# Strassen's seven block products in place of eight in a two-layer decoder's second input projection

## The chip, the core and the metric

The kernel runs on one core of one Trainium2 chip, as one program. The metric is the device time of one execution in microseconds (us). The kernel before was timed in three runs.

## What is computed

The reference is a two-layer decoder trunk on 512 tokens of width 1024, in float32. Each layer normalizes its input, mixes it (layer 0 by attention, layer 1 by a gated linear recurrence), adds the normalized result, and adds a gated embedding. The change lies where layer 0 ends and layer 1 begins:

```
gate = sigmoid(h @ ple_w_gate[0]);  h = h + (p[0] @ ple_w_proj[0]) * gate      # end of layer 0
u = rms_norm(h, norm_pre[1])                                                   # layer 1
q, fl, inp, g = split(u @ rec_w_in)          # four projections, each 512 x 1024 @ 1024 x 1024
... recurrence over chunks with q, fl, inp -> o ...
y = (rms(o) * out_gain * silu(g)) @ rec_w_out
```

`inp` (called i or `it` in the kernel) and `g` are wanted with tokens on the partitions; q and fl with channels on the partitions.

## The kernel before

All activations live in SBUF as eight tiles of 128 channels by 512 tokens. A float32 product is made of three matmuls: each operand is split into a rounded part (hi, type fp32r) and the rest (lo), and `three` (lines 138 to 142) adds hi·hi, lo·hi and hi·lo in one PSUM bank. A weight comes as a 512 KB chunk of 128 x 1024: `fetch` (L112) loads it by DMA from the SP queue into `w_raw`, a pool of three buffers; `load_w` (L117) splits it: ACT writes `w_hi` (the cast, L273), then DVE subtracts to get `w_lo` (L274). `w_hi` and `w_lo` have two buffers each, so a chunk can be split when the matmuls on the chunk two before it are done.

The end of layer 0 is `layer_tail` (L339). Its gate projection makes eight output tiles: `lin_c` (L175) makes the first four together, `lin_a` (L152) the others one after the other, 24 matmuls each, each with one chunk of `wgA`. Behind each output tile o comes `gated` (L387): ACT's sigmoid (`sgm`), DVE's product and sum into `h[o]`, and then `nxt(o)` (L401): the next layer's input is scaled by its norm's gain and split into `xg` (the tiles `b2h`, `b2l`; ACT L281, DVE L282), and ACT squares `h[o]` and DVE adds it to `ss_acc` (L222 to L230) for the norm.

Layer 1 begins with the projections i and g (lines 731 to 744). `lin_b_tok` (L188) makes a quarter of one: 512 tokens by 512 columns, four banks of 128 tokens, over eight channel tiles, with `xg` as the stationary operand and the weight as the moving one (128 x 512): 96 matmuls and four chunks of `wB1`. There are four such calls: two for i, two for g. The norm's factor per token is applied when the banks are emptied (`evac_tok`, L731). It comes from `Stat.rstd` (L248: four tiny matmuls, L236; DVE; then GpSimd's power, L252, on the engine called POOL) and is spread over the partitions for the channel-major copy `u` of the input by `spread` (L255: four matmuls, L259). `u` is made by `scaled_norm` (L285) on DVE and ACT under the products, and serves q and fl later.

Every engine runs its own instructions strictly in the order of its queue. Most of that order is chosen by a scheduler when the program is built. Under `tc.manual_schedule(engines={PE})` the order of PE's queue is that of the source. In the kernel before, the projections i and g stand outside of such a block; in the changed kernel they stand inside.

## Time and profile before

| what | value |
|---|---|
| median of three runs | 673.51 us (672.4 to 673.66) |
| the profiled execution's own time | 672.09 us |
| its span, first to last instruction | 670.3 us |
| busy share of the span: PE / DVE / ACT / POOL | 98% / 65% / 50% / 6% |
| granted TensorE clock, mean | 1.000 |
| chain that ended last: PE / DVE | 92% / 5% |
| projections i and g, first matmul of the first to last of the last | 352.89 to 441.68 us |

A busy share is a mean over stages with different limits. PE's matmuls are pipelined: one is shown as some 0.39 us long, but the next one begins before it ends, so that a stream is to be read by the distance between starts.

### The profile page before, as it was taken

To read this page: it belongs to the slowest core of one execution; us is meant where nothing else is said; L and a number is where in the kernel's file an instruction comes from. 1 tells how busy PE (TensorE), PEld (TensorE's weight loads), DVE (VectorE), ACT (ScalarE), POOL (GpSimd) and SP (SyncE) were. 2 spreads that over 40 slices of the span, in tenths; PEclk is the share of its full clock that TensorE was granted. 3 is DMA by queue.
4 is the path that set the end of the run, shared out by engine and by line. 5 is a ranking of instruction groups with operands and counts; after the bars stand their busy time and mean duration, and the time that the engine had idled before them with its cause. 6 is when DMAs were issued, how large, how long until landed. Compare 5 with 4: busy or idle time off the path is not lost.

```text
span 670.3 us, 8922 instructions
## 1 busy us (share of the span) xinstructions
PE 657.3 (98%) x3226; PEld 548.4 (82%) x3226; DVE 434.6 (65%) x893; ACT 336.9 (50%) x656; POOL 39.6 (6%) x45
## 2 busy tenths in 40 slices
PE   8999999999999998999999999999999998999996
PEld 5888888888888877888888888888888887888886
DVE  7596223888888897337694372329888888233963
ACT  6457223766767685444563453344445455433431
POOL 1102200000000061001000110000010000001000
PEclk9999999999999999999999999999999999999999
DMA  7311326655555573221223223321122124122121
GB/s 283 130 64 65 128 95 189 165 151 133 153 139 139 150 230 100 95 95 37 92 92 125 84 79 109 135 68 64 63 70 89 63 93 135 56 96 95 58 107 59
DMA packets 26578, 73.22 MB, mean 109 GB/s; under 512 B 3808, under 2 KB 4192, under 8 KB 26528
## 3 DMA queue, kind: packets, MB, share of 16 engines
q1 hardware_dynamic: 26528, 72.59, 33.9%
q8 instruction: 27, 0.44, 0.3%
q14 instruction: 23, 0.19, 0.1%
HBM read 57.76 MB, written 2.10 MB: 89 GB/s over the span
## 4 chain that ended last, share of the span: by engine, by line
PE 92%; DVE 5%; ACT 1%; DMA 1%; issue 1%; POOL 0%; SPq 0%; ACTq 0%; DVEq 0%; POOLq 0%
PE psA L140 17%; PE psA L141 17%; PE psA L142 17%; PE psB L140 7%; PE psB L142 7%; PE psB L141 7%; PE psB L638 2%; PE psB L653 1%; PE psB L615 1%; PE psB L652 1%; PE psB L614 1%; PE psA L182 1%; PE psA L183 1%; PE psA L185 1%; PE psB L183 1%; PE psB L185 1%
## 5 line engine op out<-in xcount | busy, mean ns | idle before, releaser
L274 DVE TENSOR_TENSOR w_lo<-w_raw,w_hi 128x1024 fp32r<-128x1024 f32 x91 | 111.6, 1228 | 104.1 <-ACT w_hi L273 98.8
L140 PE MATMUL psA<-b1h,w_hi 128*128 128x512 f32 (+1 forms) x384 | 154.6, 403 | 0.0
L142 PE MATMUL psA<-b1l,w_hi 128*128 128x512 f32 (+1 forms) x384 | 148.5, 387 | 0.0
L141 PE MATMUL psA<-b1h,w_lo 128*128 128x512 f32 (+1 forms) x384 | 148.2, 386 | 0.2 <-DVE w_lo L274 0.2
L273 ACT CAST w_hi<-w_raw 128x1024 fp32r<-128x1024 f32 x92 | 96.2, 1047 | 62.4 <-PE psB L141 42.1
L142 PEld LDWEIGHTS psA<-b1l,w_hi 128*128 128x128 f32 x384 | 72.1, 188 | 15.1
L140 PEld LDWEIGHTS psA<-b1h,w_hi 128*128 128x128 f32 x384 | 72.3, 188 | 12.9 <-ACT sgm L389 0.7
L141 PEld LDWEIGHTS psA<-b1h,w_lo 128*128 128x128 f32 x384 | 72.5, 189 | 12.6 <-DVE w_lo L274 0.6
L140 PE MATMUL psB<-w_hi,b2h 128*128 128x512 f32 x144 | 56.3, 392 | 0.0
L142 PE MATMUL psB<-w_lo,b2h 128*128 128x512 f32 x144 | 56.1, 389 | 0.0
L141 PE MATMUL psB<-w_hi,b2l 128*128 128x512 f32 x144 | 56.1, 389 | 0.0
L621 ACT ACTIVATE pp<-pp,nm 128x128 f32<-128x128 f32 (+3 forms) x64 | 36.2, 565 | 23.0 <-DVE nm L619 22.2
L619 DVE CUSTOM_DVE_ANT_0 pp<-psB,cmask 128x128 f32<-128x128 f32 (+3 forms) x64 | 30.7, 480 | 14.5 <-PE psB L638 11.2
L230 DVE TENSOR_TENSOR ss_acc<-ss_acc,sq 128x512 f32<-128x512 f32 x26 | 17.9, 690 | 28.9 <-ACT sq L226 28.7
L140 PE MATMUL psA<-b2h,w_hi 128*128 128x512 f32 x80 | 31.8, 397 | 0.0
L142 PEld LDWEIGHTS psB<-w_lo,b2h 128*128 128x128 f32 x144 | 27.0, 188 | 5.7
L141 PEld LDWEIGHTS psB<-w_hi,b2l 128*128 128x128 f32 x144 | 27.1, 188 | 5.5
L140 PEld LDWEIGHTS psB<-w_hi,b2h 128*128 128x128 f32 x144 | 27.0, 188 | 5.5
L274 DVE TENSOR_TENSOR PTl<-psB,PTh 128x128 fp32r<-128x128 f32 (+3 forms) x64 | 30.8, 482 | 1.0 <-ACT PTh L273 0.8
L638 PE MATMUL psB<-ident,pp 128*128 128x128 f32 x160 | 28.4, 276 | 2.9 <-DVE pp L624 1.5
L142 PE MATMUL psA<-b2l,w_hi 128*128 128x512 f32 x80 | 31.2, 390 | 0.0
L141 PE MATMUL psA<-b2h,w_lo 128*128 128x512 f32 x80 | 31.2, 390 | 0.0
(228 smaller groups left out, 1217.5 us busy)
## 6 DMA issues: line engine op xcount, KB each, us to landing
w_raw<-in_wA_dram SPq DMA_DIRECT2D x40, 512.0 KB, 3.2
w_raw<-in_wB_dram SPq DMA_DIRECT2D x23, 512.0 KB, 3.3
w_raw<-in_wo_dram SPq DMA_DIRECT2D x16, 512.0 KB, 3.8
h<-in_xT_dram SPq DMA_DIRECT2D x16, 256.0 KB, 6.0
h<-kh SPq DMA_DIRECT2D x32, 128.0 KB, 2.3
w_raw<-in_wgC_dram SPq DMA_DIRECT2D x8, 512.0 KB, 3.2
w_raw<-in_wgA_dram SPq DMA_DIRECT2D x8, 512.0 KB, 3.3
h<-qh SPq DMA_DIRECT2D x16, 128.0 KB, 2.3
```

The source lines that it names most:

```text
L140: pe.matmul(out=out_ps, lhsT=sta[0], rhs=mov[0], start=start, stop=False)
L141: pe.matmul(out=out_ps, lhsT=sta[1], rhs=mov[0], start=False, stop=False)
L142: pe.matmul(out=out_ps, lhsT=sta[0], rhs=mov[1], start=False, stop=stop)
L182: pe.matmul(out=b, lhsT=hi[:, c], rhs=src[0][k], start=k == 0, stop=False)
L183: pe.matmul(out=b, lhsT=lo[:, c], rhs=src[0][k], start=False, stop=False)
L185: pe.matmul(out=b, lhsT=hi[:, c], rhs=src[1][k], start=False, stop=k == KT - 1)
L230: ve.tensor_tensor(out=self.acc, in0=self.acc, in1=sq, op=ALU.add)
L273: ins = ac.copy(dst_hi, src)
L274: eng.tensor_tensor(out=dst_lo, in0=src, in1=dst_hi.bitcast(F32), op=ALU.subtract)
L619: ve.tensor_tensor_reduce(out=pp[:, :W], in0=sc[:, :W], in1=cmask[:, S - W:S], op0=ALU.add, op1=ALU.min, scale=1.0, scalar=-NEG, accum_out=nm)
L621: ac.activation(out=pp[:, :W], in_=pp[:, :W], func=AF.Exp, bias=nm, scale=-1.0, accum_out=den)
L638: pe.transpose(out=tp[:, kt * P:(kt + 1) * P], in_=pp[:, kt * P:(kt + 1) * P], identity=ident)
```

## The change

1. i and g, each 512 x 1024 from 512 x 1024 times 1024 x 1024, are cut into 2 x 2 blocks (256 tokens, 512 channels, 512 columns) and made of seven block products in the scheme of Strassen in Winograd's form. Each `product` is 4 channel tiles x 2 halves of 128 tokens x 3 matmuls = 24 matmuls of 128 x 512; `token_major` calls it seven times, in the order p1, p6, p7, p5, p2, p4, p3, once for i and once for g.
2. The four sums of activation blocks (D, E, F, G) are made in `pair`, called by `nxt` behind output tiles 4 to 7 of the gate projection: two ACT multiplies (`un`), four DVE sums of 128 x 256 written into a `w_raw` buffer, and a split of the 128 x 1024 into `as0k` and `as1k`. For output tiles 0 to 3, `xg` is now made for 256 tokens alone.
3. Every product has two weight chunks of its own to split: 28 chunks in place of 16. Sums of weight blocks: b11 + b12 (`t1`, in `tsum0`) and b12 + b22 come from a load by SP with an accumulating DMA behind it from POOL (`summed`); two more sums per chunk pair are made by DVE (L809, L826).
4. The results are added up from PSUM into `it` and `sg` by DVE (L796, 14 additions of 128 x 512 per projection), and scaled in place by ACT.
5. `r1` and its spread are now made between p1 and p6 of i, in PE's written order.

The diff, without empty lines:

```diff
--- before.py
+++ after.py
@@ -336,8 +336,10 @@
             with first(o == KT - 1):
                 ac.activation(out=self.zg[o], in_=b, func=AF.Copy, scale=col(C_NPOST[self.layer] + o))
 
-    def layer_tail(layer, h, ah, zg, last=False):
+    def layer_tail(layer, h, ah, zg, pair=None):
+        last = pair is None
         st = ah.st = Stat()
         ah.zg, hm = zg, ah.mem
         for g in ah.begun:
@@ -399,8 +401,12 @@
             stn = Stat()
 
             def nxt(o):
-                split_scaled(xg[0][o], xg[1][o], h[o], col(C_NPRE[1] + o))
+                f = slice(0, S // 2 if o < 4 else S)
+                split_scaled(xg[0][o][:, f], xg[1][o][:, f], h[o][:, f], col(C_NPRE[1] + o))
                 stn.add(h[o])
+                if o >= 4:
+                    pair(h, o - 4)
 
         banks = lin_c(ws, hm)
         ws = [load_w(wgA[layer, o]) for o in range(2)]
@@ -706,13 +712,33 @@
         nc.sync.dma_start(h[k], xT[:, k, :])
     att.close()
     turn[1] = 4
-    xg, st = layer_tail(0, h, ah, slots("b3h", F32))
     l1 = ctx.enter_context(tc.tile_pool(name="l1", bufs=1))
+    sums = att.enter_context(tc.tile_pool(name="sums", bufs=1))
+    TH = S // 2
+    SM_D, SM_E, SM_F, SM_G = range(4)
+    a_sum = [[sums.tile([P, 4, TH], F32R, name=f"as{q}{k}") for k in range(4)] for q in range(2)]
+    def pair(h, k):
+        un = []
+        for b in (k, k + 4):
+            un.append(t2("un"))
+            ac.mul(un[-1], h[b], col(C_NPRE[1] + b))
+        a11, a21, a12, a22 = [x[:, i * TH:(i + 1) * TH] for x in un for i in range(2)]
+        raw = wp.tile([P, D], F32, name="w_raw", tag="w_raw")
+        sm = raw.rearrange("p (j t) -> p j t", t=TH)
+        ve.tensor_tensor(out=sm[:, SM_D, :], in0=a21, in1=a22, op=ALU.subtract)
+        ve.tensor_tensor(out=sm[:, SM_E, :], in0=sm[:, SM_D, :], in1=a11, op=ALU.subtract)
+        ve.tensor_tensor(out=sm[:, SM_F, :], in0=a11, in1=a21, op=ALU.subtract)
+        ve.tensor_tensor(out=sm[:, SM_G, :], in0=a12, in1=sm[:, SM_E, :], op=ALU.add)
+        split(a_sum[0][k], a_sum[1][k], sm)
+    xg, st = layer_tail(0, h, ah, slots("b3h", F32), pair)
 
 
     lmin = const.tile([P, 1], F32, name="lmin")
@@ -728,20 +754,105 @@
     it = slots("b3h", F32)
     sg = slots("b3l", F32)
     u = pair_big("b1")
-    def evac_tok(q, banks):
-        for t in range(NT):
-            ac.activation(out=(it, sg)[q // 2][2 * t + q % 2], in_=banks[t], func=(AF.Copy, AF.Silu)[q // 2], scale=r1[:, t:t + 1])
-    banks = lin_b_tok(wB1[0:4], xg, 0)
-    r1 = st.rstd()
+    def operand(kind, k):
+        if isinstance(kind, int):
+            return [a_sum[q][k][:, kind, :] for q in range(2)]
+        row, c = kind
+        return [xg[q][k + 4 * c][:, row * TH:(row + 1) * TH] for q in range(2)]
+    def product(kind, ws):
+        banks = [psB(), psB()]
+        for k in range(4):
+            w, f = ws[k // 2], slice(k % 2 * S, (k % 2 + 1) * S)
+            hi, lo = operand(kind, k)
+            for t in range(2):
+                c = slice(t * P, (t + 1) * P)
+                three(banks[t], (hi[:, c], lo[:, c]), (w[0][:, f], w[1][:, f]), k == 0, k == 3)
+        return banks
+    def block(m, i, j, c):
+        return wB1[8 * m + 4 * j + 2 * i + c]
+    def summed(dst, *aps):
+        nc.sync.dma_start(dst, aps[0])
+        for ap in aps[1:]:
+            gp.dma_start(dst, ap, accum_op=ALU.add)
+        return dst
+    tsum = [[(l1, sums)[q].tile([P, D], F32, name=f"tsum{q}{c}", tag=f"tsum{q}{c}") for c in range(2)] for q in range(2)]
+    CH = range(2)
+    def token_major(m, dst, between=None):
+        def C(i, j, t):
+            return dst[2 * (2 * i + t) + j]
+        def plus(i, j, bank, src, op=ALU.add):
+            for t in CH:
+                ve.tensor_tensor(out=C(i, j, t), in0=bank[t], in1=C(*src, t), op=op)
+        def end(i, j):
+            for t in CH:
+                q = 2 * i + t
+                ac.activation(out=C(i, j, t), in_=C(i, j, t), func=AF.Silu if m else AF.Copy, scale=r1[:, q:q + 1])
+        w = [load_w(block(m, 0, 0, c)) for c in CH]
+        t1 = [summed(tsum[0][c], block(m, 0, 0, c), block(m, 0, 1, c)) for c in CH]
+        p1 = product((0, 0), w)
+        w = []
+        for c in CH:
+            b22 = fetch(block(m, 1, 1, c))
+            ve.tensor_tensor(out=tsum[1][c], in0=t1[c], in1=b22, op=ALU.add)
+            w.append(load_w(None, raw=tsum[1][c]))
+        if between:
+            between()
+        for t in CH:
+            ac.copy(C(0, 0, t), p1[t])
+        p6 = product(SM_E, w)
+        w = [load_w(None, raw=summed(wp.tile([P, D], F32, name="w_raw", tag="w_raw"), block(m, 0, 1, c), block(m, 1, 1, c))) for c in CH]
+        plus(0, 1, p6, (0, 0))
+        p7 = product(SM_F, w)
+        w = [load_w(None, raw=t1[c]) for c in CH]
+        plus(1, 0, p7, (0, 1))
+        p5 = product(SM_D, w)
+        w = []
+        for c in CH:
+            b21 = fetch(block(m, 1, 0, c))
+            w.append(load_w(None, raw=b21))
+            ve.tensor_tensor(out=tsum[1][c], in0=tsum[1][c], in1=b21, op=ALU.add)
+        plus(1, 1, p5, (1, 0), ALU.subtract)
+        end(1, 1)
+        plus(0, 1, p5, (0, 1), ALU.subtract)
+        p2 = product((0, 1), w)
+        w = [load_w(None, raw=tsum[1][c]) for c in CH]
+        plus(0, 0, p2, (0, 0))
+        end(0, 0)
+        p4 = product((1, 1), w)
+        w = [load_w(block(m, 1, 1, c)) for c in CH]
+        plus(1, 0, p4, (1, 0))
+        end(1, 0)
+        p3 = product(SM_G, w)
+        plus(0, 1, p3, (0, 1))
+        end(0, 1)
+    r1 = None
     rb = []
-    banks1 = lin_b_tok(wB1[4:8], xg, 1, between=lambda: rb.append(spread(r1)))
-    evac_tok(0, banks)
-    for k in range(KT):
-        scaled_norm(u, k, h[k], C_NPRE[1], rb[0])
-    evac_tok(1, banks1)
-    for q in range(2, 4):
-        evac_tok(q, lin_b_tok(wB1[4 * q:4 * q + 4], xg, q))
+    def rstd1():
+        nonlocal r1
+        r1 = st.rstd()
+        rb.append(spread(r1))
+    with tc.manual_schedule(engines={PE}):
+        token_major(0, it, rstd1)
+        for k in range(KT):
+            scaled_norm(u, k, h[k], C_NPRE[1], rb[0])
+        token_major(1, sg)
+    att.close()
 
     y = pair_big("b2")
 
@@ -749,7 +860,7 @@
         pass
 
 
-    w_f0 = load_w(wA1[8], [l1.tile([P, D], F32R, name=f"w_f0{q}") for q in range(2)])
+    w_f0 = load_w(wA1[8], [l1.tile([P, D], F32R, name=f"w_f0{q}", tag=f"tsum0{q}") for q in range(2)])
 
     def general(rp):
 
@@ -1055,7 +1166,7 @@
     with tc.If(ok > 0) as cmp:
         with tc.tile_pool(name="rec", bufs=2) as rp:
             ah = bounded(rp)
-        layer_tail(1, h, ah, it, last=True)
+        layer_tail(1, h, ah, it)
     with cmp.Else():
         with tc.tile_pool(name="rec", bufs=2) as rp:
             general(rp)
@@ -1068,7 +1179,7 @@
         for o in EARLY:
             for _ in ah.early(o):
                 pass
-        layer_tail(1, h, ah, it, last=True)
+        layer_tail(1, h, ah, it)
 
 
 _INS = ["xT", "pT", "vec", "wfl", "wA0", "wB0", "wA1", "wB1", "wo", "wgC", "wgA", "wpl"]
```

How the order of the queues changes at the places that the prediction speaks of. In the names, b2h6 is the hi part of `xg` tile 6, `sgm` the sigmoid, h7 the tile of `h`, as02 and as12 the hi and lo part of the four sums of pair 2.

DVE, in the gate projection of layer 0, from the split of its third chunk to the split of the fourth and last. Before:

```order
L274 TENSOR_TENSOR w_lo_3568<-w_raw_3565,w_hi_3567 128x1024
L391 TENSOR_TENSOR h3_2997<-h3_2997,sgm_3531 128x512
L390 TENSOR_TENSOR sgm_3571<-sgm_3571,b3l4_3369 128x512
L391 TENSOR_TENSOR h4_2998<-h4_2998,sgm_3571 128x512
L282 SCALAR_TENSOR_TENSOR b2l3_3388<-h3_2997,vecs_73,b2h3_3380 128x512
L230 TENSOR_TENSOR ss_acc_3393<-ss_acc_3393,sq_3537 128x512
L274 TENSOR_TENSOR w_lo_3608<-w_raw_3605,w_hi_3607 128x1024
```

DVE, the last ten instructions of the same piece in the changed kernel:

```order
L230 TENSOR_TENSOR ss_acc_3407<-ss_acc_3407,sq_3591 128x512
L731 TENSOR_TENSOR w_raw_3598<-un_3594,un_3596 128x256
L392 TENSOR_TENSOR sgm_3636<-sgm_3636,b3l5_3385 128x512
L732 TENSOR_TENSOR w_raw_3598<-w_raw_3598,un_3594 128x256
L393 TENSOR_TENSOR h5_2999<-h5_2999,sgm_3636 128x512
L734 TENSOR_TENSOR w_raw_3598<-un_3596,w_raw_3598 128x256
L733 TENSOR_TENSOR w_raw_3649<-un_3645 128x256
L282 SCALAR_TENSOR_TENSOR b2l5_3404<-h5_2999,vecs_73,b2h5_3396 128x512
L274 TENSOR_TENSOR as10_3021<-w_raw_3598,as00_3017 128x1024
L274 TENSOR_TENSOR w_lo_3633<-w_raw_3630,w_hi_3632 128x1024
```

Five instructions stood between the two splits; now there are fifteen, among them the four sums and the split of pair 0, the first sum of pair 1 and the output tile 5 (h5).

ACT, from the sigmoid of the last output tile of the gate projection to the first weight casts of the projections behind it (`w_hi_3781` is the second chunk of `wB1` before; `w_hi_3808` and `w_hi_3814` are the two chunks of p1 now). Before:

```order
L389 ACTIVATE sgm_3679<-psA_3654 128x512
L273 CAST w_hi_3781<-w_raw_3779 128x1024
L281 ACTIVATE b2h7_3384<-h7_3001,vecs_73 128x512
L226 ACTIVATE sq_3685<-h7_3001 128x512
L273 CAST w_hi_3811<-w_raw_3809 128x1024
```

ACT in the changed kernel:

```order
L391 ACTIVATE sgm_3726<-psA_3701 128x512
L727 ACTIVATE un_3735<-h3_2997,vecs_73 128x512
L281 ACTIVATE b2h7_3398<-h7_3001,vecs_73 128x512
L273 CAST as02_3019<-w_raw_3694 128x1024
L226 ACTIVATE sq_3732<-h7_3001 128x512
L727 ACTIVATE un_3737<-h7_3001,vecs_73 128x512
L273 CAST as03_3020<-w_raw_3739 128x1024
L273 CAST w_hi_3808<-w_raw_3806 128x1024
L273 CAST w_hi_3814<-w_raw_3812 128x1024
```

Before, the first chunk's cast stood ahead of that sigmoid and the second right behind it; now both stand behind everything that the last output tile and the pairs 2 and 3 ask of ACT, and DVE's queue has the same order (the `w_lo` of p1 behind `as13`).

PE, from the last matmuls of p1 of i to the first of p6 (`ss_acc` and `rs` belong to `r1` and its spread):

```order
L142 MATMUL psB_3823<-w_lo_3815,b2h3_3394 128x512
L236 MATMUL psB_3862<-ones1_101,ss_acc_3407 128x1 x4
L259 MATMUL psB_3871<-ident_90,rs_3869 128x128 x4
L140 MATMUL psB_3880<-w_hi_3851,as00_3017 128x512
L141 MATMUL psB_3880<-w_hi_3851,as10_3021 128x512
```

The two groups of four now stand next to each other; before, 24 matmuls of a projection stood between them.

## Rows read from the trace of the kernel before

**Rows 1.** The page, part 1: busy us (share of the span) xinstructions.

```profile
PE 657.3 (98%) x3226; PEld 548.4 (82%) x3226; DVE 434.6 (65%) x893; ACT 336.9 (50%) x656; POOL 39.6 (6%) x45
```

**Rows 2.** Timeline of PE, gate projection and first matmuls of i: start, us, instruction.

```profile
344.73 0.39 PE L140 MATMUL psA<-b1h,w_hi 128*128 128x512 f32 x1
...
347.68 0.39 PE L141 MATMUL psA<-b1h,w_lo 128*128 128x512 f32 x1
...
352.66 0.39 PE L142 MATMUL psA<-b1l,w_hi 128*128 128x512 f32 x1
352.89 0.39 PE L140 MATMUL psA<-w_hi,b2h 128*128 128x512 f32 x1
...
353.34 0.39 PE L142 MATMUL psA<-w_lo,b2h 128*128 128x512 f32 x1
```

**Rows 3.** Two stretches: us; busy PE, PEld, DVE, ACT, POOL (instructions); clock, DMA, GB/s.

```profile
331.00:353.00 22.00, 22.00 (x98) 18.24 (x98) 21.50 (x33) 15.30 (x24) 0.00 (x0) 1.00 0.21 72
354.00:441.00 87.00, 87.00 (x393) 72.23 (x392) 32.56 (x41) 32.48 (x42) 3.82 (x6) 1.00 0.29 101
```

**Rows 4.** Timeline of DVE in the gate projection.

```profile
340.29 1.22 DVE L274 TENSOR_TENSOR w_lo<-w_raw,w_hi 128x1024 fp32r<-128x1024 f32 x1
341.43 0.68 DVE L391 TENSOR_TENSOR h<-h,sgm 128x512 f32<-128x512 f32 x1
342.03 0.68 DVE L390 TENSOR_TENSOR sgm<-sgm,b3l 128x512 f32<-128x512 f32 x1
...
343.36 0.75 DVE L282 SCALAR_TENSOR_TENSOR b2l<-h,vecs,b2h 128x512 fp32r<-128x512 f32 x1
344.02 0.69 DVE L230 TENSOR_TENSOR ss_acc<-ss_acc,sq 128x512 f32<-128x512 f32 x1
344.62 1.22 DVE L274 TENSOR_TENSOR w_lo<-w_raw,w_hi 128x1024 fp32r<-128x1024 f32 x1
```

**Rows 5.** Timeline of DVE: half-width instructions at the kernel's start and end.

```profile
32.13 0.88 DVE L282 SCALAR_TENSOR_TENSOR b3h<-psA,rs,b3h 128x256 fp32r<-128x256 f32 x2 [1.42 <-ACT b3h L281]
...
665.71 0.43 DVE L390 TENSOR_TENSOR sgm<-sgm,b3l 128x256 f32<-128x256 f32 x1 [1.99 <-ACT sgm L389]
```

**Rows 6.** Timeline of ACT, the gate projection's end.

```profile
353.09 0.60 ACT L389 ACTIVATE sgm<-psA 128x512 f32<-128x512 f32 x1 [0.62 <-PE psA L142]
353.58 1.04 ACT L273 CAST w_hi<-w_raw 128x1024 fp32r<-128x1024 f32 x1
355.18 0.73 ACT L281 ACTIVATE b2h<-h,vecs 128x512 fp32r<-128x512 f32 x1 [0.55 <-DVE h L391]
355.81 0.61 ACT L226 ACTIVATE sq<-h 128x512 f32<-128x512 f32 x1
```

**Rows 7.** PE's first matmuls (L92): ns min/median/max, first and last start; then the last.

```profile
L92 PE MATMUL psB<-idle x9: 379/634/634, 1.3 to 4.5; 128*128 128x512 bf16 x9
...
L92 PE MATMUL psB<-idle x2: 379/386/393, 4.2 to 4.5; 128*128 128x512 bf16 x2
```

**Rows 8.** Timelines of DVE and POOL: the norm factor of layer 1.

```profile
375.73 0.16 DVE L239 TENSOR_SCALAR ms<-psB 128x4 f32<-128x4 f32 x1 [4.14 <-PE psB L236]
...
375.97 1.93 POOL L252 TENSOR_TENSOR rs<-ms,mhalf 128x4 f32<-128x4 f32 x1 [71.13 <-DVE ms L239]
```

**Rows 9.** Chain of waits: the two groups of small matmuls (start, us).

```profile
374.91 0.79 PE psB L236 x8
...
381.30 0.89 PE psB L259 x8
```

**Rows 10.** Timelines of ACT and DVE: one chunk's split within the projections.

```profile
363.84 1.05 ACT L273 CAST w_hi<-w_raw 128x1024 fp32r<-128x1024 f32 x1 [4.34 <-PE psB L141]
...
364.92 1.22 DVE L274 TENSOR_TENSOR w_lo<-w_raw,w_hi 128x1024 fp32r<-128x1024 f32 x1 [4.17 <-ACT w_hi L273]
```

**Rows 11.** Weight loads into w_raw, 330 to 450 us: issue ns; us to landing.

```profile
L114 SPq DMA_DIRECT2D w_raw<-in_wB_dram x16: 327/328/338, 334.1 to 417.0; - x16
...
DMA to landing us min/median/max: 3.2/3.3/4.9
```

## The prediction

> **What bounds the kernel now.** I read the page first. PE is busy for 98% of the span [rows 1], and the chain that ended last is PE for 92% of it: fewer matmuls are worth their full time as long as PE is kept fed. Next, PE's timeline: 35 matmuls lie between the starts 344.73 and 352.66 [rows 2], so one matmul of 128 x 512 costs 0.2266 us, and the stream runs into i without a gap: last matmul of the gate projection at 352.66, first of i at 352.89. Then the stretches, which decide this case: under i and g DVE is busy for 32.56 of 87.00 us, but in the gate projection, where the change puts its sums, for 21.50 of 22.00 us [rows 3]. There DVE is as full as PE; only nobody waits for it yet. A mean share of 65% doesn't show that. All sums below are against this execution's own 672.09 us, which is 1.42 us under the median of the runs shown, 673.51.
>
> **What is saved.** i and g are 4 x 96 = 384 matmuls; the change makes them 14 x 24 = 336. 48 x 0.2266 = **10.9 us** less on PE, all of it on the path. The small matmuls of the norm (0.79 and 0.89 us [rows 9]) are the same in both.
>
> **The last tile of the gate projection: 4.5 us late.** Prices on DVE, from start to start [rows 4]: 1.14 us for a chunk's split (340.29 to 341.43), 0.60 for a sum of 128 x 512 (341.43 to 342.03), 0.66 for a scaled difference (343.36 to 344.02). At half width a scaled difference is 0.40 (two in 0.88, one being 0.48 long), and a sum, 0.43 long, is 0.35, since the next begins 0.08 before its end [rows 5]. Between the splits of the third and fourth gate chunk now stand six full sums (3.6), two full and one half scaled difference (1.7), five half sums (1.75) and the split of pair 0 (1.14): 8.2 us instead of 3.2. DVE also waits for ACT three times, each time for the product of what it has itself just made: for b2h4 some 0.9 us (0.73 long [rows 6], nothing between), for b2h5 and as00 about 0.25 each, since DVE has other work meanwhile. The fourth split so begins at 340.29 + 1.14 + 8.2 + 1.4 = 351.0 and ends 1.22 later, at 352.2. PE wanted it at 347.68 [rows 2]: 4.5 us. A smaller count for the hand-overs gives 3.1, twice the count 5.9.
>
> **The entry into i: 10.2 us more.** ACT's queue puts the two casts of p1 behind everything that tile 7 and the pairs 2 and 3 ask for, though p1 reads none of it. Followed by hand, with the sigmoid of tile 7 at 353.09 + 4.5 = 357.6 [rows 6]: sigmoid to 358.2; on DVE product, one half sum of pair 2 and the sum into h7, to 359.85; ACT then makes b2h7 (0.62 to the next start), as02 (0.95), the square (0.52) and un7 (0.69), to 362.65. DVE has by then split as12 (from 361.5) and added the square, and is free at 363.25. The sums D, E and G of pair 3 each need the one before: 3 x 0.43, to 364.55. ACT: as03 0.95, then the first cast of p1, to 366.55; DVE: as13 1.14 from 365.6, then the first `w_lo` 1.22, to 368.0. So p1's third matmul begins at 368.0 where it began at 353.34 [rows 2]: 14.7 us in all, 10.2 beyond the 4.5. PE has nothing else in its order. A floor that needs no hand-over: the new work of DVE, 16 half sums (5.6) and 4 splits (4.6) less 4 x 0.26 for the halved `xg` tiles, is 9.1 us in an engine that had 0.5 us to spare; its old work ended at 357.5 (the sum after the last scaled difference), so p1's first `w_lo`, last but one in the queue, can't be done before 357.5 + 9.1 - 1.1 = 365.5: 12 us.
>
> **Clock: 1.4 us.** PE stands still for some 9 us there. The granted clock is 1.00 in both stretches [rows 3] and PE never stood that long, so the price comes from the only cold start shown: the first nine matmuls begin 0.40 apart (1.3 to 4.5), at 634 ns, and the last two take 379 to 393 [rows 7]. Eight steps at 0.40 - 0.23: 1.4 us, between nothing (the clock holds) and 2.8 (it falls in the 4.5 us wait too).
>
> **The norm factor in the open: 2.2 us.** Between p1 and p6 PE makes the means, waits for DVE (0.16) and POOL's power (1.93 [rows 8]) with nothing in between, then spreads. Before, 24 matmuls of the stream stood there. On POOL the power stands behind the issue of an accumulating DMA; by my times that has half a microsecond to spare, so 0 to 1.5 more.
>
> **Weights within the products: 3.7 us.** A chunk now lasts 12 matmuls, 2.7 us, instead of 24. Its buffer's refill takes 2.3 us (363.84 to 366.14 [rows 10]) and `w_lo` is wanted two matmuls after `w_hi`, so it fits, with 0.8 to spare, where nothing stands ahead of it. I price 26 of the 28 chunks at nothing; the cover is that spare 0.8, and without it each costs up to one addition, 0.6. Two places in g don't fit. p6: its split waits behind DVE's sums, 0.8. p7: its b12 + b22 chunk finds its buffer free only in the middle of p1. From there to p7 are 36 matmuls, 8.2 us; in it go the load 3.3 [rows 11], POOL's issue about 1 (between SP's 0.33 [rows 11] and the power's 1.93), the accumulation L, the cast 1.05 and 0.9 for the split and hand-overs: L - 2.0 late. No row shows an accumulating DMA. From below it is a plain load, 3.3; from above three of them, 10, as it reads two places and writes one. I take 5, nearer the plain one, since the slowest plain load takes 4.9 [rows 11]: 2.9 us. In i the open norm factor gives the same chunk 3.9 us more: nothing, up to an L of 6. By the fit of the Trainium skill, page "DMA: Bandwidth & Descriptors", section "Anatomy of one DMA — SWDGE (gpsimd) path" (2.0 us and the bytes at 436 GB/s), 512 KB would land in 3.2 us, an estimate: the sum would be 1.8 less; no run here shows it yet.
>
> **Costed at nothing:** the first `tsum0` loads and accumulations, which can start when attention's buffers come free and are wanted 100 us later; 14 additions per projection from PSUM (0.60 each) on a DVE that was one third busy [rows 3]; the recurrence behind, which is as before.
>
> **Sum.** -10.9 + 4.5 + 10.2 + 1.4 + 2.2 + 3.7 = **+11.1**: 683.2 against 672.09, and 684.6 as a median.
>
> **Rivals.**
> 1. *Slow accumulation.* L is 10: p7 of g loses 5 more and p7 of i 3.9: 693.5. For: POOL must prepare these while DVE is nearly always busy. Against: it hits two products only. The Trainium skill, page "SBUF — State Buffer", section "Who interferes with whom", has GpSimd and DVE lock each other out of a shared port, which would delay a descriptor written by GpSimd; it excepts sums of two tensors, DVE's main work here, by inference only.
> 2. *Not slower: the gate projection absorbs the sums.* If half sums cost DVE next to nothing and ACT hands over at once, only four splits less the halved tiles remain, 3.5 us, and the entry costs 4 in place of 14.7, with no cold clock: -10.9 + 4 + 2.2 + 2 = -2.7, 670.8. It decides at an entry of about 5 us in all (10.9 less 2.2 and 3.7). Against it: 21.50 of 22.00 busy [rows 3], and p1's casts stand behind pair 3 whatever the durations.
> 3. *DVE binds in the products.* Per projection it has 14 splits, 4 weight sums and 14 additions: 16.0 + 4.6 + 8.4 = 29.0 us for 168 matmuls, 38.1 us; in i the eight tiles of u (0.66 + 0.60 each) make it 39.1. Then up to 0.6 more at each of 14 products, 8.4: 693.0. Against: in i the wait for the norm factor gives it room, and in g 9 us are free.
>
> **How the numbers follow.** Forecast 0.71, slow accumulation 0.13, DVE in the products 0.08, absorbed sums 0.08. Low end: entry 12.0, no cold clock, L at 3.3: -10.9 + 12 + 2.2 + 1.3 = +4.6, 678; a little under it, 677. High end: the first and third rival, 693.5 and 693.0: 694. Beyond lies their coming together, and below most of the second rival. Faster or slower means by over 0.2% (1.35 us), about what a measurement of this kernel can tell. The second rival holds faster 0.05 and same 0.03; the rest is slower, 0.92.
>
> **What would show it.** Right: the first matmul of p1 some 14 us after 352.9, with ACT's `w_hi` as its releaser, and behind it the `as` splits; a wait of about 4 us in the last gate tile; one of 2 us on `rs`; from the first matmul of i to the last of g some 86 us instead of 89; slower matmuls right after the long gap. Wrong: an entry under 5 us, or a clock of 1.00 with evenly spaced matmuls all through; waits of a microsecond at most products would be the third rival, two long ones on a weight cast behind a POOL transfer the first.

## The result and the profile after

The changed kernel takes 694.29 us (median of four runs, 692.15 to 695.04) against 673.59 for the kernel before (four runs, 672.40 to 673.97): a ratio of 1.0305, 95% interval 1.0277 to 1.0333, 20.7 us slower. The sign is the predicted one; the time is 9.7 us above the forecast and 0.3 us beyond the upper end of the range. The profiled execution took 692.15 us (span 690.4), 20.06 more than that of before.

The page of the changed kernel, parts 1 and 4, to be read beside [rows 1]:

```profile
PE 658.6 (95%) x3178; PEld 544.1 (79%) x3178; DVE 485.3 (70%) x961; ACT 358.5 (52%) x684; POOL 46.5 (7%) x53
...
PE 83%; DVE 9%; DMA 3%; ACT 3%; issue 2%; POOL 1%; SPq 0%; ACTq 0%; DVEq 0%; POOLq 0%
```

PE issues 48 instructions fewer, and yet its busy time has risen by 1.3 us: some matmuls last longer. PE's share of the chain fell from 92% to 83%, and what took its place are DVE, DMA and ACT, that is, waits. Where they lie shows in PE's timeline, against [rows 2] (start, us, instruction, idle time before it and what ended it):

```profile
347.34 0.39 PE L142 MATMUL psA<-b1l,w_hi 128*128 128x512 f32 x1
350.96 0.80 PE L140 MATMUL psA<-b1h,w_hi 128*128 128x512 f32 x1 [3.24 <-ACT w_hi L273]
...
352.41 0.79 PE L141 MATMUL psA<-b1h,w_lo 128*128 128x512 f32 x1 [0.65 <-DVE w_lo L274]
353.00 0.63 PE L142 MATMUL psA<-b1l,w_hi 128*128 128x512 f32 x1
353.43 0.63 PE L140 MATMUL psA<-b1h,w_hi 128*128 128x512 f32 x1
...
359.82 0.39 PE L142 MATMUL psA<-b1l,w_hi 128*128 128x512 f32 x1
...
369.45 0.79 PE L140 MATMUL psB<-w_hi,b2h 128*128 128x512 f32 x1 [9.25 <-ACT w_hi L273]
...
370.90 0.79 PE L142 MATMUL psB<-w_lo,b2h 128*128 128x512 f32 x1 [0.23 <-DVE w_lo L274]
...
377.63 0.95 PE L236 MATMUL psB<-ones,ss_acc 128*128 128x1 f32 x8
380.90 1.82 PE L259 MATMUL psB<-ident,rs 128*128 128x128 f32 x8 [2.32 <-POOL rs L252]
...
432.19 0.62 PE L140 MATMUL psB<-w_hi,as 128*128 128x512 f32 x1 [3.19 <-ACT w_hi L273]
...
433.45 0.79 PE L142 MATMUL psB<-w_lo,as 128*128 128x512 f32 x1 [0.21 <-DVE w_lo L274]
```

There are four places where PE stands: the last gate tile, the entry into i (9.25), the norm factor (2.32) and p7 of g (3.19). Behind each, the next matmuls start 0.43 apart instead of 0.2266 (353.00 to 353.43 above). The stretches, with the columns of [rows 3], show the same from the side of the clock:

```profile
348.00:358.00 10.00, 6.38 (x15) 4.68 (x16) 9.26 (x16) 7.95 (x12) 0.00 (x0) 0.66 0.00 0
358.00:370.00 12.00, 2.75 (x11) 2.00 (x10) 8.37 (x15) 6.60 (x9) 0.00 (x0) 0.76 0.27 87
370.00:375.00 5.00, 4.77 (x13) 3.27 (x12) 3.21 (x3) 0.43 (x2) 0.00 (x0) 0.56 0.81 255
382.00:385.00 3.00, 3.00 (x11) 2.48 (x10) 2.85 (x4) 1.21 (x2) 0.00 (x0) 0.56 1.07 208
385.00:400.00 15.00, 15.00 (x66) 12.10 (x65) 12.90 (x16) 6.82 (x8) 0.84 (x1) 1.00 0.54 162
432.00:436.00 4.00, 3.60 (x8) 2.37 (x9) 1.90 (x2) 1.18 (x2) 0.00 (x0) 0.57 0.51 154
```

The third column from the right is the mean granted clock: 0.56 to 0.66 behind the waits, a mean over the lower level (1.2 GHz) and the upper one (2.4 GHz), and 1.00 once PE has run on for a while. In the first of them DVE is busy for 9.26 of 10.00 us. PE waits there for ACT's cast of the last gate chunk (3.24 us) and for DVE's split of it (0.65), and that cast stands behind the cast of `as00`, which needs DVE's sums. The end of the gate projection's queues, timelines of ACT and of DVE, shows the order that the prediction followed by hand:

```profile
367.41 1.04 ACT L273 CAST as<-w_raw 128x1024 fp32r<-128x1024 f32 x1 [2.00 <-DVE w_raw L734]
368.36 1.99 ACT L273 CAST w_hi<-w_raw 128x1024 fp32r<-128x1024 f32 x2
```

```profile
368.49 1.23 DVE L274 TENSOR_TENSOR as<-w_raw,as 128x1024 fp32r<-128x1024 f32 x1 [1.11 <-ACT as L273]
369.63 2.35 DVE L274 TENSOR_TENSOR w_lo<-w_raw,w_hi 128x1024 fp32r<-128x1024 f32 x2
```

The last sum of pair 3 releases the cast of `as03`; behind it stand p1's two casts, and on DVE p1's splits behind `as13`. Put together from start to start, against the same matmuls of before (the stream of the gate projection is 0.12 us later in this execution; that is taken off):

| place | predicted us | measured us |
|---|---|---|
| 48 matmuls fewer | -10.9 | -10.9 |
| last gate tile, wait for `w_lo` (347.68 to 352.41) | +4.5 | +4.6 |
| slow matmuls behind it (to 360.05) | 0 | +2.4 |
| entry into i, to p1's third matmul (370.90) | +10.2 | +10.4 |
| slow matmuls in p1 (to 377.63) | +1.4 | +1.7 |
| norm factor in the open (to 382.37) | +2.2 | +3.1, of which 0.7 slow |
| slow matmuls in p6 of i | 0 | +1.1 |
| p6 of g | +0.8 | +0.9 |
| p7 of g, wait for the b12 + b22 chunk | +2.9 | +4.2 |
| slow matmuls in p7 of g | 0 | +1.2 |
| products on `as`, start to start 0.2333 | 0 | +1.1 |
| the rest of i and g, less 0.4 of small waits of before | 0 | +0.1 |
| sum | +11.1 | +19.9 |

From the first `w_f` matmul on (441.90 before, 461.97 after) nothing differs.

### The profile page after: what moved, and what is told of

Same layout as the page of the kernel before. It is cut to its first block, busy times and chain, and to the rows that moved or that the text cites. A ratio compares the mean times of both kernels' runs of the same rounds, so it can differ in the third digit from the quotient of the medians.

```text
span 690.4 us, 8993 instructions
## 1 busy us (share of the span) xinstructions
PE 658.6 (95%) x3178; PEld 544.1 (79%) x3178; DVE 485.3 (70%) x961; ACT 358.5 (52%) x684; POOL 46.5 (7%) x53
## 4 chain that ended last, share of the span: by engine, by line
PE 83%; DVE 9%; DMA 3%; ACT 3%; issue 2%; POOL 1%; SPq 0%; ACTq 0%; DVEq 0%; POOLq 0%
PE psA L141 15%; PE psA L140 15%; PE psA L142 15%; PE psB L140 6%; PE psB L142 6%; PE psB L141 6%; DMA w_raw<-in_wB_dram 2%; PE psB L644 2%; DVE w_lo L274 1%; PE psB L659 1%; PE psB L621 1%; PE psB L658 1%; PE psB L620 1%; PE psA L182 1%; PE psA L183 1%
## 5 line engine op out<-in xcount | busy, mean ns | idle before, releaser
L140 PE MATMUL psB<-w_hi,b2h 128*128 128x512 f32 x96 | 38.5, 403 | 9.2 <-ACT w_hi L273 9.2
L142 PE MATMUL psB<-w_lo,b2h 128*128 128x512 f32 x96 | 38.5, 401 | 0.2 <-DVE w_lo L274 0.2
L141 PE MATMUL psB<-w_hi,b2l 128*128 128x512 f32 x96 | 38.1, 397 | 0.0
L273 ACT CAST PTh<-psB 128x128 fp32r<-128x128 f32 (+3 forms) x64 | 26.9, 422 | 5.8 <-PE psB L644 4.9
L140 PE MATMUL psB<-w_hi,as 128*128 128x512 f32 x64 | 26.6, 416 | 3.2 <-ACT w_hi L273 3.2
L140 PEld LDWEIGHTS psB<-w_hi,b2h 128*128 128x128 f32 x96 | 18.6, 193 | 13.4 <-ACT w_hi L273 9.7
```

Source lines behind the costliest of these rows:

```text
L140: pe.matmul(out=out_ps, lhsT=sta[0], rhs=mov[0], start=start, stop=False)
L141: pe.matmul(out=out_ps, lhsT=sta[1], rhs=mov[0], start=False, stop=False)
L142: pe.matmul(out=out_ps, lhsT=sta[0], rhs=mov[1], start=False, stop=stop)
L273: ins = ac.copy(dst_hi, src)
```

## The experiments

All edits are made to the changed kernel; every ratio is to the kernel before, run on the same chip.

**1. No activation sums.** What do the sums behind the gate tiles cost in all?

```diff
+    for q in range(2):
+        for k in range(4):
+            gp.memset(a_sum[q][k].bitcast(F32), 0.0)
     def pair(h, k):
-        un = []
...
-        split(a_sum[0][k], a_sum[1][k], sm)
+        pass
```

> The sums of activation blocks are left out: pair does nothing, and the as tiles are set to zero once by POOL before the gate projection, so p6, p7, p5 and p3 multiply zeros. All seven products, their weights and additions stay. Theory A (the entry is late because the sums and their splits stand ahead of the weights on DVE and ACT): the wait of 4.6 us in the last gate tile, the one of 10.4 ahead of p1 and the slow matmuls behind both (2.4 and 1.7) go, 19 us less, some 1.5 of which come back as short waits for p1's second chunk: 676 to 678 against 694.3. Rival B (the products' own weights, split by an ACT and a DVE that are behind anyway, hold p1 back): p1 still begins 4 us or more behind the last gate matmul, 682 or more. What is left over the kernel before, 673, is the price of the norm factor, of p7 in g and of the slower steps on as.

Measured: 677.10 us against 673.41, 1.0046 (1.0029 to 1.0064). The sums, with the two waits that they make and the slow matmuls behind these, are worth 17 us (694.29 - 677.10). PE runs into i without a gap; one wait is left in p1, at its second chunk:

```profile
353.43 0.39 PE L141 MATMUL psB<-w_hi,b2l 128*128 128x512 f32 x1
...
358.27 0.50 PE L142 MATMUL psB<-w_lo,b2h 128*128 128x512 f32 x1 [1.70 <-DVE w_lo L274]
```

So the saved 10.9 us are still outweighed by the norm factor and p7 of g, with the slow matmuls behind both, by that wait and by the slower products on `as`: the kernel stays 3.7 us slower than before.

**2. The sums behind p1's casts.** Was it p1's place behind the pairs, or the room for the pairs at all?

```diff
                 stn.add(h[o])
-                if o >= 4:
-                    pair(h, o - 4)
...
         w = [load_w(block(m, 0, 0, c)) for c in CH]
+        if not m:
+            for k in range(4):
+                pair(h, k)
```

> The four pairs are written behind the weight loads of p1 instead of behind the output tiles 4 to 7; order of products as in the changed kernel. Theory A (DVE and ACT have no room for the sums before p6, wherever they stand): p1 begins right behind the gate projection and costs no wait, but p6, which needs as, waits for what was moved: about 10 us there. Saved are p1's 5.4 us on PE beside the sums and one slow restart, lost again is part of it to DVE's weights for p6 standing behind the sums: about 690 against 694.3. Rival B (it is only the order of the queue: the two casts behind the pairs): the waits go without a new one, 677 or less.

Measured: 690.48 us against 673.41, 1.0271 (1.0240 to 1.0302). The two waits of the gate end are gone, and one of 10.43 us, with slow matmuls behind it, stands ahead of p6, the first product that needs a sum (PE's timeline):

```profile
362.93 1.57 PE L259 MATMUL psB<-ident,rs 128*128 128x128 f32 x8 [1.34 <-POOL rs L252]
374.93 0.79 PE L140 MATMUL psB<-w_hi,as 128*128 128x512 f32 x1 [10.43 <-ACT w_hi L273]
```

A wait was moved, not removed: p1 and the means, some 8 us of PE, don't hide the 10.2 us of sums and splits that the prediction counted on DVE, with ACT's casts in between.

**3 and 4. Idle matmuls in the waits.** Are the slow matmuls a price of the waits by themselves? PE computes nothing in its waits but is kept busy with bf16 matmuls on a constant tile, into the bank that the next product overwrites. First 13, 38, 9 and 12 of them ahead of the last gate tile, p1, the spread and p7 of g; then 18, 46, 9 and 24.

```diff
+    def busy(bank, n):
+        for _ in range(n):
+            pe.matmul(out=bank, lhsT=idle[:, 0:P], rhs=idle, start=True, stop=True)
...
         banks = [psB(), psB()]
+        busy(banks[0], n)
...
-        p1 = product((0, 0), w)
+        p1 = product((0, 0), w, 0 if m else 38)
```

> Idle matmuls (bf16, 128 x 512, of zeros, overwritten by the product that follows in the same bank) are put into PE's order where the changed kernel lets PE stand: 13 before the last gate tile, 38 before p1 of i, 9 before the spread of the norm factor, 12 before p7 of g, each count a little under the wait seen there. Nothing else is done differently. Theory A (PE's granted clock falls because PE stood still): the matmuls behind each wait begin 0.227 us apart instead of 0.43, granted clock 1.00 in all four stretches, and 2.4 + 1.7 + 1.8 + 1.2 = 7.1 us come back: about 687 against 694.3. Rival B (the matmuls behind the waits are slow because of what else restarts there, weight loads and splits): the 0.43 us steps stay, and the time stays at 694 or rises by what the idle matmuls overrun.

> The idle matmuls once more, in larger numbers, since those of the first run began 0.213 us apart and left 2.5 to 2.9 us open ahead of p1 and of p7 in g: 18, 46, 9 and 24. Theory A (granted clock falls after a pause of PE): no step of 0.43 is left behind any of the four waits, p1 of i takes 5.5 us instead of 8.2 less its own wait for w_lo, and against the first such run 1.8 + 1.3 us come back: 686.5. Rival B (the restart is slow for another reason in these two places): the steps of 0.43 stay there, 689.5.

Measured: 689.47 us against 673.05, 1.0236 (1.0213 to 1.0258), and 690.36 against 673.56, 1.0249 (1.0234 to 1.0263). In the first, the slow matmuls were gone behind the last gate tile and the spread; at p1 and p7 the idle matmuls, 0.213 us apart, ran out 2.9 and 2.5 us too early, and the slow ones stayed. In the second, no pair of product matmuls starts 0.43 apart but the first behind a filling, and the stretches of the two long waits keep a clock of 1.00 (columns of [rows 3]):

```profile
349.00:359.00 10.00, 9.95 (x45) 6.57 (x45) 9.26 (x16) 7.98 (x12) 0.00 (x0) 1.00 0.01 2
359.00:372.00 13.00, 11.95 (x53) 5.79 (x53) 10.81 (x17) 7.23 (x10) 0.00 (x0) 1.00 0.38 122
```

That shows the mechanism: ahead of p1 PE's next matmul is released by the same `w_hi` and the third by the same `w_lo` as in the changed kernel, and no slow matmuls stand behind them. It doesn't show the whole 7 us as time. By the medians the two gained 4.8 and 3.9 us on the changed kernel. The traces allow a closer count, since the gate projection's stream as a whole lies up to 2.3 us later in one execution than in another: from the end of the last gate tile but one to the first `w_f` matmul it is 114.4 us in the changed kernel, 111.7 in the first of the two and 109.8 in the second, 2.7 and 4.6 us less. In the second, 1.4 of the missing 2.5 us go at the norm factor. p1 ends earlier, but POOL's power needs DVE's `ms`, which stands behind a weight sum that waits for its load (DVE's timeline; the means began at 375.42):

```profile
376.10 1.23 DVE L816 TENSOR_TENSOR tsum<-tsum,w_raw 128x1024 f32<-128x1024 f32 x1 [2.21 <-DMA w_raw<-in_wB_dram]
...
378.38 0.15 DVE L244 TENSOR_SCALAR ms<-psB 128x4 f32<-128x4 f32 x1
```

The other 1.1 go at p7, where the 24 idle matmuls outlast the wait that they fill.

**5. p7's sum without an accumulating DMA.** b12 + b22 is (b11 + b12 + b22) - b11, and DVE has the first in `tsum1`.

```diff
-        w = [load_w(None, raw=summed(...)) for c in CH]
+        w = []
+        for c in CH:
+            b11 = fetch(block(m, 0, 0, c))
+            ve.tensor_tensor(out=b11, in0=tsum[1][c], in1=b11, op=ALU.subtract)
+            w.append(load_w(None, raw=b11))
```

> p7's weight sum b12 + b22 is made by DVE (the sum of three that it already holds, less b11, loaded once more) in place of a load and an accumulating DMA. Theory A (p7 of g waits for the accumulating DMA, 6.7 us from issue to landing, and then runs at the lower clock): the wait of 3.2 us and the second one of 0.4 go, with them 1.2 us of slow matmuls; two DVE operations of 1.23 us per projection are added under cover: about 689.5 against 694.3. Rival B (p7's chunk is late because its buffer comes free late, whoever fills it, or DVE becomes the bound): a wait of 2 us or more stays ahead of p7 of g, or new ones come at other products, 692 to 695.

Measured: 689.93 us against 673.05, 1.0243 (1.0223 to 1.0263), close to the 689.5 of theory A. The wait at p7 of g and the slow matmuls behind it are gone. But a smaller one has come at another product, as rival B had it, in p1 of g, whose first `w_lo` stands behind DVE's longer queue, and it has seven slow steps of its own:

```profile
419.63 0.79 PE L142 MATMUL psB<-w_lo,b2h 128*128 128x512 f32 x1 [2.05 <-DVE w_lo L274]
420.22 0.63 PE L140 MATMUL psB<-w_hi,b2h 128*128 128x512 f32 x1
```

**6. The means ahead of p1.** PE makes the four means before p1, so that POOL's power lies beside p1.

```diff
         t1 = [summed(tsum[0][c], ...) for c in CH]
+        if ahead:
+            ahead()
         p1 = product((0, 0), w)
```

> The four matmuls of the means (and with them DVE's and POOL's part of the norm factor) stand ahead of p1 of i, where PE waits anyway; only the spread is left between p1 and p6. Theory A (the factor's round trip stands in the open, with a slow restart behind): the 2.3 us wait goes, 0.7 of the slow spread and 1.1 of slow matmuls behind; DVE waits about 1 us for the means in the middle of pair 3, which p1's weights feel: 694.3 - 4.2 + 0.9 = 691. Rival B (what holds p6 back is its weights, and the factor's wait only hides that): p6 begins no earlier relative to the end of p1 than the 4.7 us of the changed kernel, less at most 1: 694 to 695.

Measured: 692.83 us against 673.05, 1.0291 (1.0270 to 1.0311), nearer the rival's number. p6 does follow the spread without a wait, but the long pause is cut in two, p1 begins some 1.4 us later, and its slow matmuls last longer:

```profile
367.34 1.87 PE L236 MATMUL psB<-ones,ss_acc 128*128 128x1 f32 x8 [5.97 <-DVE ss_acc L230]
372.28 0.80 PE L140 MATMUL psB<-w_hi,b2h 128*128 128x512 f32 x1 [3.07 <-ACT w_hi L273]
```

**7. `as` moved by 64 bytes.** The products on `as` start 0.2333 apart at a clock of 1.00, those on `xg` 0.2267. Is it where the tiles lie?

```diff
     l1 = ctx.enter_context(tc.tile_pool(name="l1", bufs=1))
+    l1.tile([P, 16], F32, name="pad")
```

> One unused tile of 64 bytes per partition is put ahead of the tiles of pool l1, which shifts the as tiles (and w_f0, tsum) by 64 bytes: in the changed kernel they begin at multiples of 128 bytes, while xg and w_hi, w_lo begin 64 bytes off one. The order of all queues is the same. Theory A (the pitch of 0.2333 us of the products with as, against 0.2267 of the others, goes with the place of the stationary operand): their pitch becomes 0.2267, their weight loads 188 ns instead of 197, the same for the 24 matmuls on w_f0, and 1.4 us come back: 692.9. Rival B (it goes with what DVE and the DMAs do beside these products, or with the shape of the tile): 0.2333 and 197 ns stay, 694.3.

Measured: 693.32 us against 673.05, 1.0300 (1.0275 to 1.0326); the distance stays 0.2333. That cause falls, as far as the pad did move the tiles: no trace shows where they lie. (The 197 ns of the expectation are a mean that takes in matmuls at the lower clock; see the last section.)

**8. The four sums of a pair on POOL.** Four times `gp.tensor_tensor` for `ve.tensor_tensor` in `pair`, nothing else.

```diff
-        ve.tensor_tensor(out=sm[:, SM_D, :], in0=a21, in1=a22, op=ALU.subtract)
+        gp.tensor_tensor(out=sm[:, SM_D, :], in0=a21, in1=a22, op=ALU.subtract)
...
```

> The changed kernel with one difference: the 16 sums of activation blocks in pair are made by POOL instead of DVE, at the same places. Theory A (POOL's and DVE's operations on two tensors hold each other up: a sum of 128 x 512 on DVE took 1.22 us instead of 0.69 beside POOL's in the version with sums on POOL): DVE loses about 0.5 us at each of some 15 operations between the output tiles 4 and 7 and the pairs, more than the 5.6 us taken off it; p1 of i begins 3 us or more later: 697 to 702. Rival B (the two engines don't meet): DVE's operations keep 0.69 and 1.22 us; a sum of 1 us on POOL for 0.35 on DVE makes each pair's own chain longer by what DVE's queue gets shorter: 694 give or take 1.5.

Measured: 697.92 us against 673.56, 1.0355 (1.0336 to 1.0373): slower than the changed kernel, although DVE has 16 instructions less. DVE by groups, 343 to 366 us (columns: busy us, mean ns, idle before it):

```profile
L274 DVE TENSOR_TENSOR as<-w_raw,as 128x1024 fp32r<-128x1024 f32 x3 | 3.7, 1225 | 6.7 <-ACT as L273 6.7
L392 DVE TENSOR_TENSOR sgm<-sgm,b3l 128x512 f32<-128x512 f32 x3 | 3.3, 1107 | 0.3 <-ACT sgm L391 0.3
```

Two things: sums of two tensors on DVE take 1107 ns on the mean where they took 690, and DVE now stands idle for 6.7 us for `as`, which ACT can cast only when POOL's four sums are done one after the other. The second is the larger part of the loss; the first is about 2 us.

**9. A new order, sums on POOL.** Products in the order p1, p2, p4, p6, p7, p5, p3, so that three of them need no sum of activations; the pairs' sums on POOL, their splits behind p4; the three-term weight sum by two accumulations. In this kernel the subtraction that brings p5 into two of the output blocks is written the other way round, which changes no instruction's size.

```diff
+        gp.tensor_tensor(out=d, in0=a21, in1=a22, op=ALU.subtract)
...
         p1 = product((0, 0), w)
...
+        p2 = product((0, 1), w)
...
+        p4 = product((1, 1), w)
...
         p6 = product(SM_E, w)
```

> A version of the same seven products that takes each wait by its cause. POOL makes the sums D to G while the gate projection runs; their splits come behind p4's weights. Order of products p1, p2, p4, p6, p7, p5, p3, so that the three that need no sums come first. b11 + b12 and b11 + b12 + b22 by accumulating DMAs into tiles that are free long before; b21 plus that by DVE in place; p7's sum by DVE as in the run that did so. Means of the norm factor ahead of p2, spread ahead of p4; the copy u is scaled mostly under g. POOL adds the last two terms of one block. Theory A (the loss is waits and slow restarts, nothing of it lies in the products): 10.9 us saved, less 1.3 for the slower steps on as and 2 to 4 for short waits on DVE: 673.3 - 10.9 + 4.3 = 667, between 665 and 670, PE without a wait over 2 us in i and g and the granted clock at 1.00. Rival B (DVE is full over i and g, 2 x 38 us of work in 76 us of products, and POOL's additions slow it further): waits of 0.5 us and more at most products, 672 to 680.

Measured: 684.63 us against 673.41, 1.0168 (1.0151 to 1.0185): 17.6 us over what was expected. The cover of three products was right, in that the gate projection runs without a wait. But POOL's sums slow DVE beside it, so that p1's first `w_lo` is 3.46 us late, and POOL's additions make a second wait, of 4.81 us, ahead of p3 of i: on ACT the cast of p3's weights stands behind the scaling of an output block, which waits for two additions on POOL, and these begin only at 395.93, behind a DMA issue of POOL's that waits for its load. Both waits have slow matmuls behind them (PE's timeline, then ACT's):

```profile
357.61 0.79 PE L142 MATMUL psB<-w_lo,b2h 128*128 128x512 f32 x1 [3.46 <-DVE w_lo L274]
...
400.47 0.79 PE L140 MATMUL psB<-w_hi,as 128*128 128x512 f32 x1 [4.81 <-ACT w_hi L273]
```

```profile
397.55 0.72 ACT L802 ACTIVATE b3h<-b3h,rs 128x512 f32<-128x512 f32 x1 [6.59 <-POOL b3h L843]
```

How POOL's sums slow DVE, in the timelines of the two engines:

```profile
343.58 0.69 DVE L393 TENSOR_TENSOR h<-h,sgm 128x512 f32<-128x512 f32 x1
...
347.68 1.22 DVE L392 TENSOR_TENSOR sgm<-sgm,b3l 128x512 f32<-128x512 f32 x1
...
355.81 1.74 DVE L274 TENSOR_TENSOR w_lo<-w_raw,w_hi 128x1024 fp32r<-128x1024 f32 x1
```

```profile
347.29 1.07 POOL L732 TENSOR_TENSOR sm<-sm,un 128x256 f32<-128x256 f32 x1
```

Beside a sum on POOL, DVE's 128x512 sum takes 1.22 instead of 0.69 and the 128x1024 one 1.74 instead of 1.22: some 0.53 us each, and POOL's own 1.07 instead of the 0.72 that it takes alone in experiment 8. The Trainium skill, page "SBUF — State Buffer", section "Who interferes with whom", says that a DVE instruction with both inputs in SBUF contends with GpSimd instructions that read SBUF. The traces of 8 and 9 agree, with the numbers above.

**10 and 11. The new order, sums on DVE under the products.** As 9, but POOL adds nothing and nothing is added to the gate projection: D and E are made (and E split) on ACT and DVE ahead of p6, F ahead of p7, D's split ahead of p5, G ahead of p3, and `u`, which isn't wanted before, under g. The second of the two also holds back one weight sum of g: `tsum0` for its b11 + b12 (two loads, each with an accumulating DMA behind it) is fetched only when p1 of g is done, by a one-column copy into it that reads p1's result.

```diff
-                if o >= 4:
-                    pair(h, o - 4)
...
+        p2 = product((0, 1), w)
...
+        p4 = product((1, 1), w, psA)
+        at("p6")
...
         p6 = product(SM_E, w)
+        at("p7")
...
+        token_major(0, it, dict(p2=[rstd0], p4=[rstd1], p6=[sum_de], p7=[sum_f], p5=[sum_d], p3=[sum_g]))
...
+            if m:
+                ac.copy(tsum[0][t][:, 0:1], C(0, 1, t)[:, 0:1])
```

(The last two lines stand in 11 alone.)

> The same order as in the version before (p1, p2, p4, p6, p7, p5, p3, weight sums by early accumulating DMAs, means ahead of p2 and spread ahead of p4, u scaled under g), but nothing of the additions on POOL. DVE makes the sums behind p4's weights, each only when its product is near: D and E (two operations of 128 x 256 per channel tile, from h and one scaled half) and the split of E ahead of p6, F ahead of p7, the split of D ahead of p5, G ahead of p3. p4 stays in two banks of psA until p7 is added. Theory A (POOL's additions held DVE up, and the sums are affordable where DVE has 5.4 us of products per 3.5 us of own work): 673.4 - 10.9 + 1.3 for the slower steps on as + 3 to 4 for short waits: 667, between 665 and 670, no wait over 2 us and the clock at 1.00. Rival B (DVE is full over p1 to p7 of i, whoever else is quiet): p6 and p7 wait 3 us and more, each with a slow restart, 673 or more.

> The version before with one difference: the load of t1 (b11 + b12) for g waits for a one-column copy that ACT makes behind p1 of g, so that it and its accumulating DMA move from the stretch at 384 to 400 us, where the DMA engines were fully busy (share 1.04 to 1.06, landings of 10 us), to the one at 404 to 414, where they were idle (share 0.07). Theory A (the 4.3 us that p1 and p2 of g lost went to weight loads that landed late among the accumulating DMAs): the loads of p1 and p2 of g land in some 5 us, of the 4.3 us at most 1 stays: about 669.5 against 672.9. Rival B (they were late because their buffers came free late, behind DVE's splits): p1 and p2 of g wait as before, 672 to 673.

Measured: 672.91 us against 673.56, 0.9995 (0.9984 to 1.0007), no difference; and 669.82 against 673.29, 0.9941 (0.9926 to 0.9956), 3.5 us faster than before and 24.5 faster than the change. 10 lies 6 us over its theory's 667. In it the gate projection runs without a wait and no stretch has a low clock; but i costs some 3.5 us in short waits for `w_lo` and the first products of g lose 4.3 us to loads that land late. The stretches around the entry into g:

```profile
384.00:390.00 6.00, 6.00 (x27) 4.85 (x26) 5.95 (x12) 4.31 (x8) 0.86 (x1) 1.00 1.04 270
...
396.00:402.00 6.00, 4.95 (x21) 3.42 (x19) 3.15 (x4) 2.22 (x4) 0.87 (x1) 1.00 1.06 271
```

and its DMAs in 380 to 410 us (queue 0 is POOL's, queue 1 SP's: packets, MB, share of the 16 engines' time; then the median us from issue to landing):

```profile
q0 software_dynamic: 864, 3.15, 53.4%
q1 hardware_dynamic: 1205, 4.35, 40.7%
...
tsum<-in_wB_dram POOLq DMA_DIRECT2D x5, 512.0 KB, 10.2
w_raw<-in_wB_dram SPq DMA_DIRECT2D x5, 512.0 KB, 9.9
```

Loads for later products, issued as soon as their buffers came free, fill the DMA engines for 18 us, and the chunks wanted next land 9.9 us after issue instead of 3.3 [rows 11]. Holding one of the sums back gives 3 us. The stretch at the entry into g in 11:

```profile
396.00:408.00 12.00, 11.58 (x49) 8.67 (x49) 10.43 (x13) 8.83 (x15) 0.00 (x0) 1.00 0.67 214
```

Of the 4.3 us lost in the first products of g, 1.35 stay, though the weight loads of 380 to 410 us still land 7.9 us after issue (median), not the 5 of theory A. From the first matmul of i to the last chunk's end PE now waits nowhere longer than 1.21 us. Of the 10.9 us that the seven products save, the trace of 11 has 4.6 left between the first matmul of i and the first of `w_f` (84.4 us against 89.0 before), and what follows is 1.6 longer than before (230.0 against 228.4), which no run explains.

## Why the prediction was right, and where it failed

**Right, within 0.2 us each:** the saving, the wait in the last gate tile, the entry into i, p6 of g. Following ACT's and DVE's queues by hand over the pairs gave the order in which p1's casts come, and experiment 1 shows that the sums are what it costs (17 us), experiment 2 that its place depends on the order of the queues: one wait of 10.4 us ahead of p6, in place of the two. Of the signs that the prediction named, the releaser and the order came, but p1 began 16.6 us after 352.9 instead of 14, and i and g took 92.3 us from first matmul to last instead of 86. The step named next is most of the reason for both.

**Failed: "Clock: 1.4 us".** The step took the slower clock as the price of one wait, the longest, and held a second for the upper bound, 2.8. The runs show it at each of four: 2.4 + 1.7 + 0.7 and 1.1 + 1.2 = 7.1 us, 5.7 of the 8.8 that are missing. Two things went wrong. The step asked whether the clock falls at all, from a trace in which PE never stood, and having found a price for the gap of 9 us did not apply it to the gaps of 4.5, 2.2 and 2.9 that the same text had worked out. And it took the length of the slow piece from the nine matmuls of the cold start [rows 7]: in the last gate tile there are ten steps of 0.43 and one of 0.59. The trace of experiment 4 shows that these are the clock and not late data. The Trainium skill, page "TensorE: Matmul & The Clock Gate", section "HAM oscillation — how this bites in real kernels", describes a kernel that pays for the slow restart at every one of its waits, not once; the trace agrees at these four, with 1.1 to 2.4 us per wait. As time, 3 and 4 gave back 2.7 and 4.6 of the 7.1 us in their traces: in 3 the slow matmuls at p1 and p7 stayed, and in 4 2.5 us went to later waits.

**Mis-sized: "p7 ... L - 2.0 late", L = 5.** The form was right. POOL's issue at 424.09 ended at 424.94 and the cast that it released began at 431.09, an L of 6.2, and 6.2 - 2.0 is the measured 4.2. (The terms that the step lists add up to L - 1.9, and to 3.1 us at its own L of 5, where it wrote 2.9.) The DMA view of the changed kernel, 360 to 462 us, has 6.7 and 8.3 us from issue to landing where the plain loads have 4.8:

```profile
q1 hardware_dynamic: 3658, 13.30, 39.5%
q0 software_dynamic: 864, 3.15, 17.6%
...
w_raw<-in_wB_dram SPq DMA_DIRECT2D x19, 512.0 KB, 4.8
w_raw<-in_wB_dram POOLq DMA_DIRECT2D x4, 512.0 KB, 6.7
...
tsum<-in_wB_dram POOLq DMA_DIRECT2D x2, 512.0 KB, 8.3
```

The 3.2 us that the fit in the Trainium skill, page "DMA: Bandwidth & Descriptors", section "Anatomy of one DMA — SWDGE (gpsimd) path", gave as an estimate is half of what is measured: here the measurement decides. Experiment 5 takes the accumulation away, and with it the wait. From the end of the last gate tile but one to the first `w_f` matmul it is 3.4 us shorter than the changed kernel: 5.4 less at p7 (4.2 and 1.2), 0.7 at p6 of g and some 0.8 at the norm factor, where POOL's power took 1.01 us instead of 1.97 (why is not shown; it took 1.93 in the kernel before), against some 3.7 more in p1 of g, the new wait of 2.05 and the slow steps behind it. Rival 1 (L of 10) did not come: p7 of i waits for nothing.

**Not in the sum:** the pitch of the products on `as` (1.1 us). The trace of the kernel before has the same pitch at one place that the prediction did not read: the 24 matmuls on `w_f`, 16 steps of 0.233 from 442.14 to 445.87.

**The rivals.** Absorbed sums are refuted by the entry of 15 us. DVE binding in all products is refuted too: p2 and p4 of i lose nothing, and p3 0.16, which is that pitch. **The range** was too narrow for one main reason: its upper end was built from the rivals, each with the forecast's one restart. Three more at the forecast's own 1.4 us would have made the forecast 688.8 and the upper end 698, with the result inside.

## What to carry to other kernels

A saving on the engine that bounds the span is worth its time only if the work that it creates lands where another engine has room: read the stretch, not the mean share, and when a kernel is slowed in this way move the added work under products that need none of it, as in experiment 11. Price each long wait of PE twice, once for its length and once for the slow matmuls behind it; the waits of 1.70 us in experiment 1 and of 1.21 in experiment 11 had none behind them. And when buffers come free earlier, look at what loads start then: the one wanted last can hold up the one wanted next.

## What the runs showed of the hardware

- Sums of two tensors on DVE and sums on POOL slow each other: DVE 0.69 to 1.22 and 1.22 to 1.74 us, POOL 0.72 to 1.07 (experiments 8 and 9).
- The accumulating DMAs took more of the DMA engines' time than their bytes: 17.6% for 3.15 MB against 39.5% for 13.30 MB of plain loads, which is 1.9 times as much per byte; in experiment 10 it is 1.8 times. They are also the only ones on POOL's queue here, so the runs don't tell the accumulation from the queue.
- Products whose stationary tile is `as` start 0.2333 us apart at a clock of 1.00, as do those on `w_f` in the kernel before. Their weight loads take no longer than those of `xg`: 188 ns each (PE's weight loads of the changed kernel, 386 to 431 us, mean ns in the second column).

```profile
L141 PEld LDWEIGHTS psB<-w_hi,as 128*128 128x128 f32 x36 | 6.8, 188 | 1.6
...
L141 PEld LDWEIGHTS psB<-w_hi,b2l 128*128 128x128 f32 x24 | 4.5, 188 | 1.0
```

The 197 ns that the expectation of experiment 7 starts from is the mean of 382 to 481 us, in which p6 of i and p7 of g run in part at the lower clock. The pitch comes from neither the clock, nor a shift by 64 bytes (experiment 7), nor the values, since it stays with `as` all zero (experiment 1), nor the length of the weight loads. What it comes from stays open.
